# Expert weights laid out by the host, one solid piece of 8 KB per partition and load

## The chip, the cores and the metric

The kernel runs on one core of a Trainium2 chip. The metric is the device time of the whole program in microseconds, the median of three runs. The engines are TensorE (PE, with its weight loads as PEld), VectorE (DVE), ScalarE (ACT), GpSimd (POOL) and SyncE (SP). SP issues every DMA of this kernel; 16 DMA engines carry them.

## The reference

256 tokens of 1024 numbers, all float32, pass through two blocks. The first has a conditioned norm, a mixer (convolution and mLSTM) and a mixture of 32 experts; the second has two layers of attention and a SwiGLU network. The experts are the part that matters here:

```python
def expert_rows(args):
    xb, e = args
    return (jax.nn.silu(xb @ w_e_gate[e]) * (xb @ w_e_up[e])) @ w_e_down[e]
```

`w_e_gate` and `w_e_up` have 1024 x 512 numbers per expert, `w_e_down` 512 x 1024: 6 MB per expert, 192 MB in all, and every expert's weights are read once. Each token goes to two experts; which ones, a router computes on the chip.

## The kernel before

The program is one function, `tile_two_blocks_kernel`. All large weights come in loads of 1 MB into tiles called `raw` of 128 partitions x 2048 numbers. `load` (line 64) takes a buffer and issues the DMA from SP (line 69); `load_k` (line 72) cuts rows `k0*128` to `(k0+k)*128` and `n` columns out of a matrix, with the rows `k*128+p` on partition p.

For the experts, `part` (line 703) calls `load_k`. A gate or up load takes half an expert's matrix, 4 x 128 rows of 512 numbers; each partition gets four pieces of 2 KB that stand 256 KB apart in memory. A down load takes 2 x 128 rows of 1024 numbers: two pieces of 4 KB per partition. That is six loads of 1 MB for each expert, 192 in all. In the stage of the experts there are 16 `raw` buffers, in three pools that take turns (line 691).

Experts are worked in units (`UNITS`, line 36): four units of two experts, then six of four. The first four experts are fixed, the later ones are taken in the order `order`, which is computed on the chip, so from then on SP reads the expert's number into a register (line 700) and the DMA's address comes from it. `load_to` (line 721) issues loads up to 16 ahead of the unit that is worked. For each unit TensorE does `gather` (line 891, every second unit), `gate_up` (line 913, tiles pg and pu), a transpose, `down` (line 954, tile pd), and then `combine` into acc. A group of loads is free when its matmuls are done, and SP waits for that buffer by buffer.

Ahead of the third unit stands `fallback()` (line 850): a branch (line 853) that all engines take, over a loop for the case that an expert got more tokens than its unit has room for. The loop reads the same weights in pieces of its own (lines 871 and 878).

Tiles and tensors in the rows: `raw<-in_w_e_gate_dram` is such a load; xg, pg, pu, hT, pd, acc are the unit's tiles; `in_ada_w_dram` and `in_a_w_qkv_dram` are weights of the second block, loaded by the same `load`.

Of the kernel before, what the change touches and what calls it, by code (L numbers as in the profile page):

```python
# [7 lines left out]
F32 = mybir.dt.float32  # L8
# [12 lines left out]
NE = 32  # L21
# [21 lines left out]
def kernel(ctx: ExitStack, tc: tile.TileContext, I, cst, out):  # L43
    nc = tc.nc
    PE, ACT, DVE, POOL, SP = nc.tensor, nc.scalar, nc.vector, nc.gpsimd, nc.sync
# [10 lines left out]
    def pb(name):  # L56
        return psum.tile([128, 512], F32, name=name, tag="pb", bufs=3)
# [6 lines left out]
    def load(src, k, n):  # L64
        pick = pools["raw"][pools["n"] % len(pools["raw"])]
        pools["n"] += 1
        t = pick.tile([128, 2048], F32, name="raw", tag="raw")
        v = t[:, :k * n].rearrange("p (k n) -> p k n", n=n)
        pools.get("dma", SP).dma_start(out=v, in_=src)  # L69
        return v  # L70

    def load_k(w, k0, k, n0, n):
        return load(w[k0 * 128:(k0 + k) * 128, n0:n0 + n].rearrange("(k p) n -> p k n", p=128), k, n)
# [49 lines left out]
    def mm(o, a, b, first=True, last=True):  # L123
        return PE.matmul(o, a, b, start=first, stop=last, skip_group_check=True)  # L124
# [473 lines left out]
    for i in range(2):  # L598
        ps = pa("hmT")
        for j in range(2):  # L600
            h = 2 * i + j
            for t in range(2):
                PE.transpose(ps[:, j * 256 + t * 128:j * 256 + (t + 1) * 128], hm[:, t, h, :], ident)
            src = ps[:, j * 256:(j + 1) * 256]
# [84 lines left out]
    with tc.tile_pool(name="moe", bufs=1) as pp, \  # L689
# [5 lines left out]
        def expert_loads():  # L695
            for ne, r0 in UNITS:
                w = ewt[r0] = [{}, {}, {}]
                for r in range(r0, r0 + ne):
                    if r not in at:
                        at[r] = nc.values_load(order[0:1, r:r + 1], engines=[mybir.EngineType.SP], min_val=0, max_val=NE - 1,  # L700
                                               skip_runtime_bounds_check_because="a permutation of the experts")

                def part(i, nm, k0, k, n, j):
                    e = at[r0 + j]
                    src = I[nm][0][e] if isinstance(e, int) else I[nm][0][bass.ds(e, 1)].rearrange("e k n -> (e k) n")
                    w[i][k0 // k, j] = load_k(src, k0, k, 0, n)

                for h in range(2):
                    for i, nm in enumerate(("w_e_gate", "w_e_up")):
                        for j in range(ne):  # L710
                            part(i, nm, 4 * h, 4, 512, j)
                            yield
                for h in range(2):
                    for j in range(ne):
                        part(2, "w_e_down", 2 * h, 2, 1024, j)
                        yield

        loads = expert_loads()
        loaded = [0]

# [129 lines left out]
        def fallback():  # L850
            over = nc.values_load(ovi, min_val=0, max_val=1,
                                  skip_runtime_bounds_check_because="a comparison gives zero or one")
            with tc.If(over > 0, preferred_fallthrough_block=False):
                wide = pp.tile([64, 33], F32, name="wide")
                DVE.tensor_scalar(wide[:, 32:33], place, WIDE - 0.5, float(CAP4), op0=ALU.is_lt, op1=ALU.mult)
                DVE.tensor_scalar(wide[0:32, 0:32], ident[0:32, 0:32], wide[0:32, 32:33], None, op0=ALU.mult)
                pw = pb("ovw")[:, 0:32]
                mm(pw, ones[0:32, :], wide[0:32, 0:32])
                wov = pp.tile([128, 2, 32], F32, name="wov")
                for t in range(2):  # L860
                    DVE.tensor_tensor(wov[:, t, :], sl[:, t, :], pw, ALU.subtract)
                    DVE.scalar_tensor_tensor(wov[:, t, :], wov[:, t, :], CAP4 + 0.5, wE[:, t, :], op0=ALU.is_gt, op1=ALU.mult)
                ov = pp.tile([128, 2048], F32, name="ov", tag="xg", bufs=2)
                hid = ov[:, 0:1024].rearrange("p (f t) -> p f t", f=4)
                wg = ov[:, 1024:2048].rearrange("p (k n) -> p k n", n=128)
                wd = ov[:, 1024:1536].rearrange("p (k n) -> p k n", n=128)
                with tc.For_i(0, NE, 1) as e:
                    for f in range(4):
                        ps = pb("ovgu")
                        for j, nm in enumerate(("w_e_gate", "w_e_up")):  # L870
                            SP.dma_start(out=wg, in_=I[nm][0][bass.ds(e, 1), :, f * 128:(f + 1) * 128]
                                         .rearrange("e (k p) n -> p (e k) n", p=128))
                            for k in range(KT):
                                mm(ps[:, j * 256:(j + 1) * 256], wg[:, k, :], h32[:, k, :], k == 0, k == KT - 1)
                        ACT.activation(hid[:, f, :], ps[:, 0:256], AF.Silu)
                        DVE.tensor_tensor(hid[:, f, :], hid[:, f, :], ps[:, 256:512], ALU.mult)
                    for n in range(8):
                        SP.dma_start(out=wd, in_=I["w_e_down"][0][bass.ds(e, 1), :, n * 128:(n + 1) * 128]
                                     .rearrange("e (k p) n -> p (e k) n", p=128))
                        for t in range(2):  # L880
                            ps = pb("ovd")
                            for k in range(4):
                                mm(ps[:, 0:128], hid[:, k, t * 128:(t + 1) * 128], wd[:, k, :], k == 0, k == 3)
                            tmp = pp.tile([128, 512], F32, name="ovt", tag="yl", bufs=2)[:, 0:128]
                            DVE.tensor_tensor(tmp, ps[:, 0:128], gate2[:, n * 128:(n + 1) * 128], ALU.mult)
                            xs = x[:, t, n * 128:(n + 1) * 128]
                            DVE.scalar_tensor_tensor(xs, tmp, wov[:, t, bass.ds(e, 1)], xs, op0=ALU.mult, op1=ALU.add)
# [94 lines left out]
        for u, (ne, r0) in enumerate(UNITS):  # L982
            if u == 2:
                fallback()
                gf = act.tile([128, D], F32, name="gf", tag="gate1")
                SP.dma_start(out=gf, in_=I["g_final"].unsqueeze(0).to_broadcast([128, D]))
            done += 6 * ne
            load_to(done + RAW_BUFS + RAW2_BUFS)
            if u % 2 == 0:
                gr, xg = gather(u)  # L990
            g = slice(128 * (u % 2), 128 * (u % 2) + 128)
            hid = gate_up(ne, ewt[r0], xg[:, :, g])
            if prev:
                prev()
            gT, ws = scatter_of(ne, r0, gr[:, :, g])
            prev = down(ne, ewt[r0], transposed(hid), gT, ws, u == 0, u == len(UNITS) - 1)
            ewt.pop(r0)
# [364 lines left out]
def _constants():  # L1362
# [27 lines left out]
    def ang(pos, half, theta):  # L1390
# [10 lines left out]
    return c  # L1401


_INS = ["x", "c", "w_ada", "b_ada", "g_norm1", "w_in", "b_if", "conv_dw_w", "conv_dw_b", "conv_ln_g", "conv_ln_b",
        "w_conv_out", "qk_conv_w", "qk_conv_b", "m_norm_g", "w_m_out", "w_out", "g_norm2", "w_rg", "b_rg", "w_re",
        "b_re", "w_e_gate", "w_e_up", "w_e_down", "g_final", "c_2", "ada_w_2", "ada_b_2", "norm1_g_2", "norm2_g_2",
        "a_w_qkv_2", "a_w_o_2", "a_lam_q1_2", "a_lam_k1_2", "a_lam_q2_2", "a_lam_k2_2", "a_subln_g_2", "b_w_qkv_2",
        "b_w_o_2", "b_qnorm_g_2", "b_knorm_g_2", "f_w_in_2", "f_w_out_2", "final_g_2"]

# [20 lines left out]
```

## Time and profile before

| | us |
|---|---|
| median of 3 runs | 1456.59 (1455.54 to 1457.0) |
| the profiled execution | 1455.63 |
| its span, first to last instruction | 1453.9 |

The mean granted clock of TensorE in the profiled execution is 0.956 of full speed. The profile comes from one execution; spans and sums are made against 1455.63. Times in the rows below are microseconds from the start of the span. The share of the DMA engines is the time that packets took, over 16 engines; overlapping packets can bring it above 1.

### The profile page before, as it was taken

To read this page: it belongs to the slowest core of one execution; us is meant where nothing else is said; L and a number is where in the kernel's file an instruction comes from. 1 tells how busy PE (TensorE), PEld (TensorE's weight loads), DVE (VectorE), ACT (ScalarE), POOL (GpSimd) and SP (SyncE) were. 2 spreads that over 40 slices of the span, in tenths; PEclk is the share of its full clock that TensorE was granted. 3 is DMA by queue.
4 is the path that set the end of the run, shared out by engine and by line. 5 is a ranking of instruction groups with operands and counts; after the bars stand their busy time and mean duration, and the time that the engine had idled before them with its cause. 6 is when DMAs were issued, how large, how long until landed. Compare 5 with 4: busy or idle time off the path is not lost.

```text
span 1453.9 us, 20075 instructions
## 1 busy us (share of the span) xinstructions
PE 1303.4 (90%) x8125; PEld 888.7 (61%) x8125; DVE 620.3 (43%) x1074; ACT 490.9 (34%) x840; POOL 57.9 (4%) x99
## 2 busy tenths in 40 slices
PE   5799999897997787777778999999999999999997
PEld 1686797634342222121125877698999777799997
DVE  0798856511111011010016545754544765744454
ACT  1465354311010000010006555543443554643442
POOL 0000000000000000000002211000000120000000
PEclk9899999798999899898999999999999999999999
DMA  8987557899999999999999766658555566755500
GB/s 303 401 290 260 197 185 257 310 409 360 392 409 410 414 406 414 410 411 414 408 390 337 257 229 207 244 187 290 174 175 173 203 216 212 285 188 184 174 30 30
DMA packets 200002, 408.83 MB, mean 281 GB/s; under 512 B 10057, under 2 KB 90430, under 8 KB 193762
## 3 DMA queue, kind: packets, MB, share of 16 engines
q1 hardware_dynamic: 199906, 407.51, 76.1%
q8 instruction: 65, 1.06, 0.3%
q14 instruction: 31, 0.25, 0.0%
HBM read 406.43 MB, written 1.05 MB: 280 GB/s over the span
## 4 chain that ended last, share of the span: by engine, by line
PE 74%; DMA 15%; DVE 4%; SPq 3%; issue 2%; ACT 2%; POOL 1%; POOLq 0%; DVEq 0%; ACTq 0%
PE ada L124 5%; DMA raw<-in_w_e_up_dram 5%; PE pu L124 5%; PE pd L124 4%; DMA raw<-in_w_e_down_dram 4%; PE pg L124 4%; PE fu L119 3%; PE fg L120 3%; PE fg L119 3%; PE fg L121 3%; PE fu L120 3%; PE fu L121 3%; PE facc L119 3%; DMA raw<-in_w_e_gate_dram 3%; SPq L69 3%; PE facc L120 3%
## 5 line engine op out<-in xcount | busy, mean ns | idle before, releaser
L92 DVE TENSOR_TENSOR lo<-raw,hi 128x1024 fp32r<-128x1024 f32 x120 | 145.2, 1230 | 126.3 <-ACT hi L90 124.6
L110 DVE TENSOR_TENSOR lo<-raw,hi 128x1024 fp32r<-128x1024 f32 x120 | 146.1, 1224 | 97.0 <-ACT hi L108 96.8
L90 ACT ACTIVATE hi<-raw 128x1024 fp32r<-128x1024 f32 x120 | 125.0, 1061 | 143.9 <-PE facc L121 79.2
L108 ACT ACTIVATE hi<-raw 128x1024 fp32r<-128x1024 f32 x120 | 125.8, 1057 | 123.6 <-issue 55.8
L124 PE MATMUL pu<-raw,xg 128*32 128x512 f32 (+1 forms) x512 | 130.2, 744 | 31.3 <-DMA raw<-in_w_e_up_dram 31.3
L124 PE MATMUL pd<-raw,hT 128*32 128x512 f32 (+1 forms) x512 | 111.1, 597 | 16.7 <-DMA raw<-in_w_e_down_dram 8.8
L124 PE MATMUL pg<-raw,xg 128*32 128x512 f32 (+1 forms) x512 | 109.6, 622 | 17.4 <-DMA raw<-in_w_e_gate_dram 17.4
L926 DVE TENSOR_TENSOR hid<-hid,pu 128x256 f32<-128x256 f32 x20 | 7.5, 418 | 241.9 <-PE pu L124 241.9
L119 PE MATMUL fg<-Hh,lo 128*128 128x256 f32 x352 | 100.7, 286 | 4.3 <-DVE Hh L351 4.3
L124 PE MATMUL ada<-raw,cc 128*32 128x512 f32 x576 | 98.0, 635 | 6.5 <-DMA raw<-in_w_ada_dram 6.5
L124 PEld LDWEIGHTS pu<-raw,xg 128*32 128x32 f32 (+1 forms) x512 | 30.3, 138 | 117.4 <-DMA raw<-in_w_e_up_dram 63.2
L120 PE MATMUL fg<-Hl,hi 128*128 128x256 f32 x352 | 100.4, 285 | 0.9 <-DVE Hl L115 0.9
L119 PE MATMUL fu<-Hh,lo 128*128 128x256 f32 x352 | 100.8, 286 | 0.0
L121 PE MATMUL fg<-Hh,hi 128*128 128x256 f32 x352 | 100.3, 285 | 0.0
L120 PE MATMUL fu<-Hl,hi 128*128 128x256 f32 x352 | 100.3, 285 | 0.0
L121 PE MATMUL fu<-Hh,hi 128*128 128x256 f32 x352 | 100.2, 285 | 0.0
L119 PE MATMUL dense<-hi,Hl 128*128 128x256 f32 x288 | 82.9, 288 | 0.1
L124 PEld LDWEIGHTS pd<-raw,hT 128*32 128x32 f32 (+1 forms) x512 | 30.3, 116 | 84.5 <-issue 58.0
L120 PE MATMUL dense<-lo,Hh 128*128 128x256 f32 x288 | 81.5, 283 | 0.0
L121 PE MATMUL dense<-hi,Hh 128*128 128x256 f32 x288 | 81.4, 284 | 0.0
L124 PEld LDWEIGHTS pg<-raw,xg 128*32 128x32 f32 (+1 forms) x512 | 26.6, 120 | 77.6 <-issue 41.4
L119 PEld LDWEIGHTS fg<-Hh,lo 128*128 128x128 f32 x352 | 68.2, 194 | 6.5 <-issue 4.7
(413 smaller groups left out, 2608.6 us busy)
## 6 DMA issues: line engine op xcount, KB each, us to landing
raw<-in_w_e_gate_dram SPq DMA_DIRECT2D x64, 1024.0 KB
raw<-in_w_e_up_dram SPq DMA_DIRECT2D x64, 1024.0 KB
raw<-in_w_e_down_dram SPq DMA_DIRECT2D x64, 1024.0 KB
raw<-in_ada_w_dram SPq DMA_DIRECT2D x48, 1024.0 KB
raw<-in_f_w_in_dram SPq DMA_DIRECT2D x44, 1024.0 KB
raw<-in_w_ada_dram SPq DMA_DIRECT2D x24, 1024.0 KB
raw<-in_f_w_out_dram SPq DMA_DIRECT2D x22, 1024.0 KB
raw<-in_w_in_dram SPq DMA_DIRECT2D x20, 1024.0 KB
```

Of the source, the lines that this page charges most:

```text
L69: pools.get("dma", SP).dma_start(out=v, in_=src)
L90: ACT.activation(hv, src, AF.Copy)
L92: DVE.tensor_tensor(lv, src, hv.bitcast(F32), ALU.subtract)
L108: ACT.activation(hv, src, AF.Copy)
L110: DVE.tensor_tensor(lv, src, hv.bitcast(F32), ALU.subtract)
L119: PE.matmul(o, al, bh, start=first, stop=False, skip_group_check=True)
L120: PE.matmul(o, ah, bl, start=False, stop=False, skip_group_check=True)
L121: PE.matmul(o, ah, bh, start=False, stop=last, skip_group_check=True)
L124: return PE.matmul(o, a, b, start=first, stop=last, skip_group_check=True)
L926: DVE.tensor_tensor(hid[:, c], hid[:, c], pgu[1][:, c], ALU.mult)
```

## The change

The host builds one array `experts` of (32, 6, 128, 2048) numbers instead of passing the three weight arrays: for each expert the two halves of gate, of up and of down, each already in the form of the tile, so that partition p's 2048 numbers stand in one piece of 8 KB, and a load's 1 MB in one piece too. `part` then loads one such block, into the same tile with the same meaning of its columns. The fallback loop reads its smaller pieces out of the same array, in two halves.

```diff
-                def part(i, nm, k0, k, n, j):
+                def part(i, h, j):
                     e = at[r0 + j]
-                    src = I[nm][0][e] if isinstance(e, int) else I[nm][0][bass.ds(e, 1)].rearrange("e k n -> (e k) n")
-                    w[i][k0 // k, j] = load_k(src, k0, k, 0, n)
+                    src = I["experts"][bass.ds(e, 1), 2 * i + h].rearrange("e p (k n) -> (e p) k n", k=2 if i == 2 else 4)
+                    w[i][h, j] = load(src, src.shape[1], src.shape[2])
...
-                            SP.dma_start(out=wg, in_=I[nm][0][bass.ds(e, 1), :, f * 128:(f + 1) * 128]
-                                         .rearrange("e (k p) n -> p (e k) n", p=128))
+                            for h in range(2):
+                                SP.dma_start(out=wg[:, 4 * h:4 * h + 4, :], in_=I["experts"][bass.ds(e, 1), 2 * j + h]
+                                             .rearrange("e p (k n) -> (e p) k n", k=4)[:, :, f * 128:(f + 1) * 128])
...
+def _experts(inputs):
...
+    parts = []
+    for name, k in (("w_e_gate", 4), ("w_e_up", 4), ("w_e_down", 2)):
+        w = np.asarray(inputs[name])[0]
+        parts.append(w.reshape(NE, 2, k, 128, -1).transpose(0, 1, 3, 2, 4).reshape(NE, 2, 128, 2048))
+    return np.ascontiguousarray(np.concatenate(parts, axis=1))
```

On TensorE, VectorE, ScalarE and GpSimd the order of instructions is the same before and after, row for row. On SP the loads keep their places and waits. The first place is SP at the branch of the fallback, with the waits of each row (DMAHW are the landings of SP's own loads, PE is TensorE). Before:

```order
L69 DMA raw<-in_w_e_gate_dram 128x4x512 [waits DMAHW0_49,PE_49]
L69 ISA
L69 DMA raw<-in_w_e_up_dram 128x4x512 [waits DMAHW1_49,PE_49]
L69 ISA
L69 DMA raw<-in_w_e_up_dram 128x4x512 [waits DMAHW2_49,PE_49]
L851 TENSOR_LOAD ovi [waits DVE_49]
L853 COMPARE_AND_BRANCH
L853 UNCONDITIONAL_BRANCH [waits DMAHW0_49,DMAHW1_49,DMAHW2_49,DMAHW3_49,DMAHW4_49,DMAHW5_49,DMAHW6_49,DMAHW7_49]
```

And now:

```order
L69 DMA raw<-experts_dram 128x2048 [waits DMAHW0_49,PE_49]
L69 ISA
L69 DMA raw<-experts_dram 128x2048 [waits DMAHW1_49,PE_49]
L69 ISA
L69 DMA raw<-experts_dram 128x2048 [waits DMAHW2_49,PE_49]
L851 TENSOR_LOAD ovi [waits DVE_49]
L853 COMPARE_AND_BRANCH
L853 UNCONDITIONAL_BRANCH [waits DMAHW0_49,DMAHW1_49,DMAHW2_49,DMAHW3_49,DMAHW4_49,DMAHW5_49,DMAHW6_49,DMAHW7_49]
```

Nothing moved: each load has the same waits, and its destination has become one piece of 2048 numbers per partition. In both, SP leaves the branch only when all its eight landing counters stand where they should.

The second place is SP inside the fallback loop (tile ov), which a run enters only when an expert overflows. Before:

```order
L871 DMA ov<-in_w_e_gate_dram 128x8x128 [waits DMAHW3_49,DVE_49,Activation_49]
L871 ISA
L871 DMA ov<-in_w_e_up_dram 128x8x128 [waits DMAHW4_49,DMAHW3_49,PE_49]
L871 ISA
L871 DMA ov<-in_w_e_gate_dram 128x8x128 [waits DMAHW5_49,DMAHW4_49,PE_49]
```

And now:

```order
L872 DMA ov<-experts_dram 128x4x128 [waits DMAHW3_49,DVE_49,Activation_49]
L872 ISA
L872 DMA ov<-experts_dram 128x4x128 [waits DMAHW4_49]
L872 ISA
L872 DMA ov<-experts_dram 128x4x128 [waits DMAHW5_49,DMAHW3_49,PE_49]
```

Each load of the loop has become two of half the size.

## Rows read from the trace of the kernel before

**Rows 1.** The page: busy tenths, DMA and GB/s in 40 slices of the span.

```profile
PE   5799999897997787777778999999999999999997
DMA  8987557899999999999999766658555566755500
GB/s 303 401 290 260 197 185 257 310 409 360 392 409 410 414 406 414 410 411 414 408 390 337 257 229 207 244 187 290 174 175 173 203 216 212 285 188 184 174 30 30
```

**Rows 2.** The chain that ended last, expert stage: start us, us, what.

```profile
336.91 14.24 DMA raw<-in_w_e_gate_dram
...
362.74 0.42 PE pg L124
...
375.65 7.09 PE pd L124 x32
...
400.03 7.09 PE pd L124 x32
...
428.15 3.01 PE pu L124 x21
431.16 17.76 DMA raw<-in_w_e_down_dram
...
722.66 13.26 DMA raw<-in_w_e_up_dram
```

**Rows 3.** Windows of the expert stage; the last columns are granted clock, DMA share, GB/s.

```profile
356.00:358.00 2.00, 2.00 (x12) 1.87 (x13) 0.00 (x0) 0.89 (x3) 0.00 (x0) 0.61 1.02 396
358.00:360.00 2.00, 2.00 (x8) 0.61 (x7) 0.00 (x0) 0.86 (x2) 0.00 (x0) 1.00 0.47 180
360.00:362.00 2.00, 2.00 (x12) 0.87 (x13) 0.76 (x2) 0.56 (x1) 0.00 (x0) 1.00 0.11 41
362.00:364.00 2.00, 2.00 (x12) 0.71 (x10) 0.00 (x0) 0.00 (x0) 0.00 (x0) 1.00 0.11 15
364.00:368.00 4.00, 4.00 (x22) 1.30 (x20) 0.00 (x0) 0.00 (x0) 0.00 (x0) 1.00 0.87 306
...
460.00:478.00 18.00, 12.83 (x60) 2.52 (x52) 0.00 (x0) 0.00 (x0) 0.00 (x0) 0.81 1.05 407
740.00:752.00 12.00, 9.72 (x53) 2.68 (x46) 1.44 (x3) 0.00 (x0) 0.00 (x0) 1.00 1.02 418
```

**Rows 4.** Timeline of SP, its load issues: start us, us with waits, what, count.

```profile
362.75 1.03 SPq L69 DMA_DIRECT2D raw<-in_w_e_gate_dram  x2
...
397.48 8.61 SPq L69 DMA_DIRECT2D raw<-in_w_e_gate_dram  x4
```

**Rows 5.** DMA issues between 230 and 362 us.

```profile
raw<-in_w_e_gate_dram SPq DMA_DIRECT2D x14, 1024.0 KB
raw<-in_w_e_up_dram SPq DMA_DIRECT2D x14, 1024.0 KB
raw<-in_w_e_down_dram SPq DMA_DIRECT2D x12, 1024.0 KB
```

**Rows 6.** DMA queue (packets, MB, share of 16 engines) and issues between 362.5 and 740 us.

```profile
q1 hardware_dynamic: 65483, 153.79, 103.5%
...
raw<-in_w_e_down_dram SPq DMA_DIRECT2D x52, 1024.0 KB
raw<-in_w_e_gate_dram SPq DMA_DIRECT2D x50, 1024.0 KB
raw<-in_w_e_up_dram SPq DMA_DIRECT2D x50, 1024.0 KB
```

**Rows 7.** DMA packets in 460 to 478 us, 430 to 446 us, 44 to 60 us.

```profile
DMA packets 3687, 7.32 MB, mean 407 GB/s; under 512 B 112, under 2 KB 112, under 8 KB 3687
...
DMA packets 1742, 6.73 MB, mean 421 GB/s; under 512 B 98, under 2 KB 98, under 8 KB 1742
...
DMA packets 3599, 6.52 MB, mean 408 GB/s; under 512 B 98, under 2 KB 3189, under 8 KB 3189
```

**Rows 8.** One window with few loads in flight, those of ada weights in 8 KB pieces.

```profile
227.00:231.00 4.00, 4.00 (x37) 4.00 (x36) 1.57 (x3) 0.86 (x2) 0.00 (x0) 1.00 0.99 371
```

More of the change, by code (lines that the diff above doesn't have):

```diff
@@ L701, in expert_loads @@
                                                skip_runtime_bounds_check_because="a permutation of the experts")
-                def part(i, nm, k0, k, n, j):
+                def part(i, h, j):
                     e = at[r0 + j]
-                    src = I[nm][0][e] if isinstance(e, int) else I[nm][0][bass.ds(e, 1)].rearrange("e k n -> (e k) n")
-                    w[i][k0 // k, j] = load_k(src, k0, k, 0, n)
+                    src = I["experts"][bass.ds(e, 1), 2 * i + h].rearrange("e p (k n) -> (e p) k n", k=2 if i == 2 else 4)
+                    w[i][h, j] = load(src, src.shape[1], src.shape[2])
                 for h in range(2):
-                    for i, nm in enumerate(("w_e_gate", "w_e_up")):
+                    for i in range(2):
                         for j in range(ne):
-                            part(i, nm, 4 * h, 4, 512, j)
+                            part(i, h, j)
                             yield
@@ L714, in expert_loads @@
                     for j in range(ne):
-                        part(2, "w_e_down", 2 * h, 2, 1024, j)
+                        part(2, h, j)
                         yield
@@ L869, in fallback @@
                         ps = pb("ovgu")
-                        for j, nm in enumerate(("w_e_gate", "w_e_up")):
-                            SP.dma_start(out=wg, in_=I[nm][0][bass.ds(e, 1), :, f * 128:(f + 1) * 128]
-                                         .rearrange("e (k p) n -> p (e k) n", p=128))
+                        for j in range(2):
+                            for h in range(2):
+                                SP.dma_start(out=wg[:, 4 * h:4 * h + 4, :], in_=I["experts"][bass.ds(e, 1), 2 * j + h]
+                                             .rearrange("e p (k n) -> (e p) k n", k=4)[:, :, f * 128:(f + 1) * 128])
                             for k in range(KT):
@@ L877, in fallback @@
                     for n in range(8):
-                        SP.dma_start(out=wd, in_=I["w_e_down"][0][bass.ds(e, 1), :, n * 128:(n + 1) * 128]
-                                     .rearrange("e (k p) n -> p (e k) n", p=128))
+                        for h in range(2):
+                            SP.dma_start(out=wd[:, 2 * h:2 * h + 2, :], in_=I["experts"][bass.ds(e, 1), 4 + h]
+                                         .rearrange("e p (k n) -> (e p) k n", k=2)[:, :, n * 128:(n + 1) * 128])
                         for t in range(2):
@@ L1401, in _constants @@
     return c
+def _experts(inputs):
+    import numpy as np
+    parts = []
[3 more added lines that the diff above has]
+    return np.ascontiguousarray(np.concatenate(parts, axis=1))
 _INS = ["x", "c", "w_ada", "b_ada", "g_norm1", "w_in", "b_if", "conv_dw_w", "conv_dw_b", "conv_ln_g", "conv_ln_b",
         "w_conv_out", "qk_conv_w", "qk_conv_b", "m_norm_g", "w_m_out", "w_out", "g_norm2", "w_rg", "b_rg", "w_re",
-        "b_re", "w_e_gate", "w_e_up", "w_e_down", "g_final", "c_2", "ada_w_2", "ada_b_2", "norm1_g_2", "norm2_g_2",
+        "b_re", "g_final", "c_2", "ada_w_2", "ada_b_2", "norm1_g_2", "norm2_g_2",
         "a_w_qkv_2", "a_w_o_2", "a_lam_q1_2", "a_lam_k1_2", "a_lam_q2_2", "a_lam_k2_2", "a_subln_g_2", "b_w_qkv_2",
@@ L1422 @@
         aps[name] = nc.dram_tensor(f"in_{name}_dram", a.shape, mybir.dt.from_np(a.dtype), kind="ExternalInput").ap()
+    arrays["experts_dram"] = _experts(inputs)
+    aps["experts"] = nc.dram_tensor("experts_dram", (NE, 6, 128, 2048), F32, kind="ExternalInput").ap()
     arrays["constants_dram"] = _constants()
```

## Prediction

> **What bounds the kernel now.** I read the page first, then the stages by window, then the chain of waits, and last the DMA queue in the few stretches where one size of piece moves alone. [rows 1] shows two kinds of stage. In slices 9 to 21 of 40 (36.3 us each, the experts) the DMA engines show 9 and move 390 to 414 GB/s, but for slice 10 with 360, while PE shows mostly 7; from slice 23 on PE shows 9 and DMA drops to 5 to 8. So a cheaper load can pay in the expert stage alone. TensorE over the whole span (90%) tells nothing about that stage.
>
> The expert stage is itself three stretches.
>
> - *283 to 345 us.* The chain is TensorE with almost no break; the first 16 loads were fetched ahead. A faster load is not waited for here. The step "DMA raw<-in_w_e_gate" at 336.91, 14.24 us long, ends at 351.15, where PE goes on with the next gather [rows 2]; a gather reads no weights, and before it PE stands in the branch of line 853. I count that step as the branch, not as a load.
> - *345 to 364 us.* SP also meets that branch, and there it waits for every load that it has issued (first order piece above). DMA runs dry: 396, 180, 41 and 15 GB/s in four steps of 2 us [rows 3]. SP's next load goes out at 362.75 [rows 4], and the chain has TensorE's matmuls pg ending at 362.74 [rows 2]: it is a buffer freed by TensorE that it waited for. After this TensorE is the chain without a break until 431 [rows 2].
> - *364 to some 752 us.* DMA is never idle: its queue's share is 103.5% of 16 engines from 362.5 to 740 us [rows 6], 1.05 and 1.02 in two windows of it [rows 3] (packets overlap a little, so a full engine reads over 1). From 431 the chain hangs on loads that take 13 to 18 us from issue to landing, because they stand behind others [rows 2]. Here the time is the number of loads times the time of one. [rows 6] counts them: 52 down, 50 gate and 50 up; with the 40 before [rows 5] that is all 192.
>
> After the last down load there are PE's last matmuls, the norms and the second block; the order of instructions on all engines is the same there, so this tail simply follows.
>
> **What one piece costs.** Between 460 and 478 us only gate and up loads move: 3687 packets, 112 of them small, so 3575 pieces of 2 KB in 18 us. 16 engines x 18,000 ns / 3575 = 80.6 ns for a piece. Between 430 and 446 only down loads: 1742 - 98 = 1644 pieces of 4 KB in 16 us, 155.7 ns each [rows 7]. The second 2 KB cost 75.1 ns, the first 80.6: a piece costs about 5.5 ns and then 75.1 ns for 2 KB. Drawn on to 8 KB: 155.7 + 2 x 75.1 = 305.9 ns. A load of 1 MB in 128 pieces gives every engine 8, so 2.447 us, against 32 x 80.6 = 2.579 us for gate and up and 16 x 155.7 = 2.491 us for down.
>
> The trace holds 8 KB pieces too (the ada weights), never alone in a full queue. Between 44 and 60 us they mix with 1 KB pieces: 3599 packets, 3189 under 2 KB, of which 98 are small, so 3091 of 1 KB and 410 of 8 KB [rows 7]. With 43.0 ns for 1 KB (the same line drawn back), 256 us of engine time less 132.9 leaves 300 ns for a piece of 8 KB. I take the cheap bound from it: 300 ns, a load of 2.40 us. The dear bound is that nothing is gained past 4 KB: 2 x 155.7 = 311.4 ns, 2.491 us. I take 305.9, which lies between.
>
> The Trainium skill, page "DMA: Bandwidth & Descriptors", section "Specifications", gives 512 B as the smallest transfer for line rate. By that rule 2 KB pieces lose nothing and the change brings 0 us. [rows 7] does not agree: 407 GB/s with 2 KB and 421 with 4 KB in full queues.
>
> **The change part by part.**
>
> - *Gate and up loads, 100 of them in the full stretch:* 2.579 - 2.447 = 0.132 us each, 13.2 us.
> - *Down loads, 52:* 2.491 - 2.447 = 0.044 us each, 2.3 us.
> - *The 40 loads before 362 us* (28 gate and up, 12 down [rows 5]): they get cheaper by at most 28 x 0.132 + 12 x 0.044 = 4.2 us, and I count none of it. The cover is TensorE's chain, unbroken by loads up to 431 [rows 2]; the queue only runs dry some 4 us sooner, at about 356, and then waits for the same buffer at 362.75. Without that cover the whole 4.2 us would be gained.
> - *SP's own time.* Four issues take SP 8.61 us in the full stretch, 2.2 us each, and two take 1.03 us where the queue is empty [rows 4]. Fewer pieces may let SP run further ahead, up to its 16 buffers. That moves no byte sooner while the engines are full: 0 us. Its waits and its order are the same (first order piece).
> - *The fallback loop* gets 32 loads per expert where 16 were (second order piece). It is skipped in this run: the 192 loads of [rows 5, 6] are all there are. 0 us.
> - *TensorE's side:* the same matmuls on the same numbers. Its own pace is shown where it did not wait: from 375.65 to 400.03, one unit of 12 loads in 24.4 us [rows 2], 2.03 us a load. That unit has two experts; it stays under 2.447. So loads stay what is waited for.
>
> Sum: 13.2 + 2.3 = 15.5 us. The profiled execution took 1455.63 us (span 1453.9 and 1.7 around it), 0.96 under the median of the three runs. 1455.63 - 15.5 = 1440.1; set against the median, 1441.1 us.
>
> A measurement of this kernel tells about 0.2% (2.9 us) from no change.
>
> **The rivals.** Their times are set against the median.
>
> - *No gain past 4 KB.* A piece of 8 KB would cost as two of 4 KB. Then gate and up gain 100 x (2.579 - 2.491) = 8.8 us, down nothing: 1447.8 us. For it speaks that no stretch has 8 KB pieces alone at the full rate; against it the mixed stretch of [rows 7], which left no more than 300 ns. The Trainium skill, same page, section "Why small descriptors are slow (HBM only)", names a fixed cost of about 3 cycles for each packet beside one for each 32 B. By it (an estimate: 67, 131 and 259 cycles for 2, 4 and 8 KB) gate and up would gain 3.4%, down 1.1%, together some 10 us, near this rival; [rows 7] shows a larger fixed cost, 5.5 ns of 80.6.
> - *The early loads pay too, or 8 KB is cheaper still.* If SP at 362.75 waited for its own loads (it does wait for them in the branch) and TensorE's end at 362.74 only fell together with it, the 4.2 us come on top: 1436.9. With 300 ns a piece instead of 305.9 (2.400 us a load) the sum is 100 x 0.179 + 52 x 0.091 = 22.6 us: 1434.0. Against the first: TensorE's chain runs on past 362 with no wait for a load.
> - *Slower: long pieces that start 8 KB apart read worse.* Every load becomes one solid MB, and the 16 engines walk it side by side. No load of before has that shape. The slowest rows with 8 KB pieces are 227 to 231 us, 371 GB/s at a share of 0.99 [rows 8]: 1.0486 MB / 371 GB/s = 2.826 us a load, and 152 x 2.826 - (100 x 2.579 + 52 x 2.491) = +42 us, so 1498.6. The point where it decides: a mean load of 387.4 / 152 = 2.549 us, 411 GB/s. Against it: at 227 us there were few loads in the queue, 2 KB pieces go at 306 in such a place too (364 to 368 [rows 3]), and down loads read a solid stretch already, at 421.
> - *No change:* 1456.6. It needs something other than the loads to set the stretch from 431 on; the DMA share of 103.5% [rows 6] speaks against it. The first rule cited above would give this time.
>
> **How the numbers follow.** The forecast (1438.5 to 1444.5) has 0.62; the early loads or a cheaper piece 0.13; no gain past 4 KB 0.12; no change 0.05; slower 0.08. Faster is 0.62 + 0.13 + 0.12 = 0.87, same 0.05, slower 0.08. For the range I leave out the slow case, no change, and the far end of the cheap one: 1436 to 1448.5 holds the forecast, most of the next and the 4 KB case. The prediction is that of the likeliest case, 1441.1.
>
> **What the next profile would show.** Right: DMA at 425 to 430 GB/s with a share near 1.02 in the stretch from some 364 us to the end of the expert loads; that end near 737 instead of 752; 128 packets of 8 KB per load; the dry spot at 356 to 364 a few us longer, and SP's next load again at about 362.7; TensorE's waits for loads 2.45 us apart; the time from the last down load to the end unchanged. The first step is wrong if the full stretch stays at 421 or falls under 411; the step on the early loads is wrong if SP's load after the branch goes out at 359 or before. The prediction as a whole fails if DMA shows gaps in the full stretch, which would mean that buffers, not bytes, set the pace.

## The result, and the profile after

The changed kernel took 1440.8 us (median of 4 runs, 1440.68 to 1442.87) against 1456.07 for the kernel before (4 runs, 1455.43 to 1457.0): a ratio of 0.9889, 95% interval 0.9876 to 0.9903. Forecast were 1441.1 us and 1436 to 1448.5. The changed kernel was profiled again later beside other runs of before: 1444.55 against 1455.91, ratio 0.9918 (0.9906 to 0.9931). So the gain is 15.3 us by the first pair of medians and 11.4 by the second; what lies between is taken up below.

The slices of the page after (TensorE, DMA, GB/s, then the packets of the whole execution) answer to [rows 1]. In slices 12 to 20, counted from 1 as in the prediction, DMA now moves 425 or 426 GB/s, where it moved 406 to 414; the packets are 142,658.

```profile
PE   5799999897997777677769999999999999999997
...
DMA  8987557798899999999989666757554665855500
GB/s 303 403 287 258 196 193 264 305 415 374 375 426 425 426 425 426 426 426 425 426 347 366 225 216 224 261 185 273 172 194 144 223 226 195 297 185 176 175 30 30
DMA packets 142658, 408.83 MB, mean 284 GB/s; under 512 B 10057, under 2 KB 90430, under 8 KB 111842
```

Windows of the expert stage after (the last three columns are granted clock, DMA share and GB/s) answer to [rows 3]:

```profile
354.00:356.00 2.00, 2.00 (x10) 2.00 (x11) 0.00 (x0) 0.86 (x2) 0.00 (x0) 0.50 0.82 340
356.00:358.00 2.00, 2.00 (x11) 2.00 (x11) 0.00 (x0) 1.03 (x3) 0.00 (x0) 0.50 0.19 74
358.00:360.00 2.00, 2.00 (x10) 0.74 (x9) 0.00 (x0) 1.29 (x3) 0.00 (x0) 0.99 0.00 0
360.00:362.00 2.00, 2.00 (x11) 1.02 (x12) 0.76 (x2) 0.57 (x1) 0.00 (x0) 1.00 0.01 4
362.00:364.00 2.00, 2.00 (x14) 0.58 (x10) 0.00 (x0) 0.00 (x0) 0.00 (x0) 1.00 0.10 16
364.00:368.00 4.00, 4.00 (x22) 1.43 (x20) 0.00 (x0) 0.00 (x0) 0.00 (x0) 1.00 0.89 358
...
460.00:478.00 18.00, 10.78 (x52) 2.35 (x56) 0.00 (x0) 0.00 (x0) 0.00 (x0) 0.89 1.01 425
500.00:600.00 100.00, 76.16 (x388) 21.48 (x388) 8.94 (x21) 5.93 (x12) 0.00 (x0) 0.93 1.01 425
```

The dry spot is longer and starts sooner: counted against this kernel's full rate of 426 GB/s it loses some 8.6 us of DMA time; the one in [rows 3], counted against the 407 there, loses 5.9. It still ends at the same moment. SP's next load, on its timeline (start, us with waits, what, count), goes out 0.16 us later than in [rows 4]:

```profile
362.91 1.18 SPq L69 DMA_DIRECT2D raw<-experts_dram  x2
```

The DMA queue from 362.5 to 740 us answers to [rows 6], a third of the packets for the same loads (two loads of a_w_qkv and one of ada_w come with them):

```profile
q1 hardware_dynamic: 22135, 159.49, 100.4%
...
raw<-experts_dram SPq DMA_DIRECT2D x152, 1024.0 KB
```

The chain of waits after, beside [rows 2]:

```profile
336.29 15.06 DMA raw<-experts_dram
...
352.03 1.83 PE gath L124 x7
...
407.67 0.57 PE gath L124 x4
408.24 17.59 DMA raw<-experts_dram
...
702.95 19.55 DMA raw<-experts_dram
...
722.62 19.57 DMA raw<-experts_dram
...
742.23 3.64 PE pd L124 x20
```

TensorE is the chain up to 408 us; from there it is loads, but for one stretch of 20 us from 485 on, a unit's down and the next gather. Two steps on loads start 19.67 us apart, and SP has 8 loads under way by then: 2.459 us a load, where 2.447 was forecast.

**Three marks.** To tell where a difference lies I read three moments in every trace: the first matmul on expert weights (tile pg, 64 columns), the first one of the fifth unit (pg, 32 columns), and the start of the last one on expert weights (pd). Up to the fifth unit a unit has two experts, from there four. The lines give min/median/max ns and the first and last start. Before:

```profile
L124 PE MATMUL pg<-raw,xg x16: 592/592/643, 289.3 to 294.5; 128*64 128x512 f32 x16
...
L124 PE MATMUL pg<-raw,xg x34: 592/592/617, 412.1 to 420.3; 128*32 128x512 f32 x34
...
L124 PE MATMUL pd<-raw,hT x64: 589/592/617, 743.7 to 758.9; 128*32 128x512 f32 x64
```

After:

```profile
L124 PE MATMUL pg<-raw,xg x16: 592/592/706, 289.6 to 294.9; 128*64 128x512 f32 x16
...
L124 PE MATMUL pg<-raw,xg x34: 592/592/617, 412.7 to 420.8; 128*32 128x512 f32 x34
...
L124 PE MATMUL pd<-raw,hT x35: 592/592/617, 734.6 to 745.3; 128*32 128x512 f32 x35
```

The table has the same for all kernels of this study, from one profile each; A is the first mark, A to B and B to C the stretches between marks, and the rest is the span behind C.

| kernel | A | A to B | B to C | A to C | rest |
|---|---|---|---|---|---|
| before | 289.3 | 122.8 | 346.8 | 469.6 | 695.0 |
| changed | 289.6 | 123.1 | 332.6 | 455.7 | 695.8 |
| after_again (changed, second profile) | 290.2 | 122.8 | 332.9 | 455.7 | 694.8 |
| gate_up_only | 287.6 | 123.4 | 334.6 | 458.0 | 696.7 |
| down_only | 288.4 | 123.0 | 344.4 | 467.4 | 695.4 |
| pieces_2k | 289.5 | 122.4 | 354.6 | 477.0 | 696.7 |
| pieces_4k | 287.7 | 123.0 | 338.1 | 461.1 | 696.7 |
| far_pitch | 292.2 | 122.9 | 332.6 | 455.5 | 695.0 |
| early_old | 291.4 | 122.3 | 334.8 | 457.1 | 696.4 |
| early_new | 289.7 | 123.0 | 346.5 | 469.5 | 695.3 |
| before_no_fallback | 287.7 | 119.9 | 343.4 | 463.3 | 698.5 |
| after_no_fallback | 290.8 | 120.1 | 330.8 | 450.9 | 696.8 |
| fallback_pool | 289.6 | 123.0 | 332.6 | 455.6 | 696.8 |
| fallback_u6 | 293.8 | 123.7 | 338.9 | 462.6 | 695.4 |

From A to C the change gains 13.9 us, in both profiles of the changed kernel, and all of it behind B.

### The profile page after: what moved, and what is told of

Same layout as the page of the kernel before. It is cut to its first block, busy times and chain, and to the rows that moved or that the text cites. A ratio compares the mean times of both kernels' runs of the same rounds, so it can differ in the third digit from the quotient of the medians.

```text
span 1441.1 us, 20075 instructions
## 1 busy us (share of the span) xinstructions
PE 1292.9 (90%) x8125; PEld 889.5 (62%) x8125; DVE 620.7 (43%) x1074; ACT 491.0 (34%) x840; POOL 58.0 (4%) x99
## 4 chain that ended last, share of the span: by engine, by line
PE 67%; DMA 25%; DVE 3%; issue 2%; ACT 1%; POOL 1%; SPq 0%; POOLq 0%; DVEq 0%; ACTq 0%
DMA raw<-experts_dram 23%; PE ada L124 6%; PE fg L120 3%; PE fu L119 3%; PE fg L119 3%; PE fg L121 3%; PE fu L120 3%; PE fu L121 3%; PE facc L119 3%; PE facc L120 3%; PE facc L121 3%; PE pd L124 2%; PE dense L119 2%; PE dense L120 2%; PE dense L121 2%; PE pu L124 2%
## 5 line engine op out<-in xcount | busy, mean ns | idle before, releaser
L108 ACT ACTIVATE hi<-raw 128x1024 fp32r<-128x1024 f32 x120 | 125.9, 1057 | 122.3 <-issue 55.8
L124 PE MATMUL pu<-raw,xg 128*32 128x512 f32 (+1 forms) x512 | 108.7, 638 | 29.8 <-DMA raw<-experts_dram 29.8
L124 PE MATMUL pg<-raw,xg 128*32 128x512 f32 (+1 forms) x512 | 117.5, 690 | 17.5 <-DMA raw<-experts_dram 17.5
L966 DVE SCALAR_TENSOR_TENSOR pd<-pd,ws,gate 128x512 f32<-128x512 f32 x20 | 15.2, 759 | 133.1 <-PE pd L124 132.1
```

Of the source, the lines that this page charges most:

```text
L108: ACT.activation(hv, src, AF.Copy)
L966: DVE.scalar_tensor_tensor(pd, pd, ws, gate2[:, n * 512:(n + 1) * 512], op0=ALU.mult, op1=ALU.mult)
```

## The experiments

The theory at the start: the time of the full stretch is the number of pieces times the cost of a piece, and a piece costs a few ns whatever its length. The first rivals: it is not the length but the order in memory; or the single array; or that SP can run further ahead.

**gate_up_only and down_only: one part of the change each.** Gate and up alone from the new array:

```diff
-                    src = I["experts"][bass.ds(e, 1), 2 * i + h].rearrange("e p (k n) -> (e p) k n", k=2 if i == 2 else 4)
-                    w[i][h, j] = load(src, src.shape[1], src.shape[2])
+                    if i < 2:
+                        src = I["experts"][bass.ds(e, 1), 2 * i + h].rearrange("e p (k n) -> (e p) k n", k=2 if i == 2 else 4)
+                        w[i][h, j] = load(src, src.shape[1], src.shape[2])
+                    else:
+                        src = I["w_e_down"][0][bass.ds(e, 1)].rearrange("e k n -> (e k) n")
+                        w[i][h, j] = load_k(src, 2 * h, 2, 0, 1024)
```

> Gate and up from the new array in 8 KB pieces, down from its own array in 4 KB pieces as before. Theory (the time of the full stretch is the number of pieces times the cost of a piece): 100 x 0.132 = 13.2 us of the gain stay, so 1442.9 us; worked from the changed kernel's 1440.8 and its measured 2.4715 us a load, 52 x (2.491 - 2.4715) = 1.0 us is lost, 1441.8. Rival (what helps is that one array with one pitch holds all loads, or that SP can run ahead all the time): with every third load of the old kind a good part of the 15 us is lost, 1446 or more.

Measured: 1443.47 us, ratio to before 0.9913 (0.9895 to 0.9932), before 1456.4 in this set. A to C is 11.6 us shorter than before. down_only is the same edit the other way round:

> Down from the new array in 8 KB pieces, gate and up from their own arrays in 2 KB pieces as before. Theory: 52 x 0.044 = 2.3 us gained, 1453.8 us (by the measured 2.4715 us a load only 1.0 us, 1455.1). Rival (SP's running ahead or the single array is what helps): 1450 or less.

Measured: 1456.01 us, ratio 0.9988 (0.9976 to 1.0); A to C 2.2 us shorter. The two parts add up, 11.6 + 2.2 = 13.8 to the whole 13.9, and each stands near its term (13.2 and 2.3). The rival that a mixture loses the gain falls. In the medians down_only shows hardly anything: 2 us is less than runs of one kernel differ.

**pieces_2k and pieces_4k: the length of a piece alone.** In pieces_2k the host leaves 512 B free after every 2 KB of a row, so that no two blocks are neighbours; in pieces_4k it stores a tile as two halves. The load's destination is written in as many pieces (not shown).

In pieces_2k:

```diff
-                    src = I["experts"][bass.ds(e, 1), 2 * i + h].rearrange("e p (k n) -> (e p) k n", k=2 if i == 2 else 4)
+                    src = I["experts"][bass.ds(e, 1), 2 * i + h].rearrange("e p b n -> (e p) b n")[:, :, 0:512]
...
-    return np.ascontiguousarray(np.concatenate(parts, axis=1))
+    w = np.concatenate(parts, axis=1).reshape(NE, 6, 128, 4, 512)
+    return np.concatenate([w, np.zeros((NE, 6, 128, 4, 128), w.dtype)], axis=4)
```

In pieces_4k:

```diff
-                    src = I["experts"][bass.ds(e, 1), 2 * i + h].rearrange("e p (k n) -> (e p) k n", k=2 if i == 2 else 4)
+                    src = I["experts"][bass.ds(e, 1), 2 * i + h].rearrange("e b p n -> (e p) b n")
...
-        parts.append(w.reshape(NE, 2, k, 128, -1).transpose(0, 1, 3, 2, 4).reshape(NE, 2, 128, 2048))
+        parts.append(w.reshape(NE, 2, k, 128, -1).transpose(0, 1, 3, 2, 4).reshape(NE, 2, 128, 2, 1024).transpose(0, 1, 3, 2, 4))
```

> The changed kernel's order in memory, but each row of 8 KB is cut in four by gaps of 512 B, so that all 152 loads of the full stretch, down too, move in pieces of 2 KB. Theory: 152 x 2.579 us instead of 152 x 2.4715, 16.3 us more than the changed kernel, 1457; counted from the kernel before, 52 x (2.579 - 2.491) = 4.6 us more, 1460.7. Full stretch near 407 GB/s, 80 to 81 ns a piece. Rival (the order in memory, all of a partition's numbers side by side, is what helps, not the length of a piece): 1441 to 1444.

> Each load is two solid halves of 512 KB, 4 KB per partition in each, so that all 152 loads of the full stretch move in pieces of 4 KB. Theory with the predicted line (305.9 ns for 8 KB, 155.7 for 4): 152 x 0.044 = 6.7 us more than the changed kernel, 1447.5. Theory with the measured 2.4715 us a load: 152 x (2.491 - 2.4715) = 3.0 us more, 1443.8. Rival (no gain past 4 KB): 1441, as the changed kernel.

Measured: pieces_2k 1464.33 us, ratio to before 1.0044 (1.0028 to 1.0061), slower than before; pieces_4k 1449.08, ratio 0.9945 (0.993 to 0.996). From A to C pieces_4k takes 5.4 us more than the changed kernel, between its two theories (6.7 and 3.0). pieces_2k misses its expectation (1457, or 1460.7 counted from before): from A to C it takes 21.3 us more than the changed kernel and 7.4 more than before. Some 3.4 us of both lie at the branch, where SP's next load goes out 76.8 us behind A, in the kernel before 73.5 and in the changed one 73.3:

```profile
366.37 0.58 SPq L70 DMA_DIRECT2D raw<-experts_dram  x1
```

SP leaves the branch there at 363.4; for the 3 us up to this issue the profile shows no wait, and what fills them stays open. The other 4 us against before are about what the down loads now cost more, 52 x (2.576 - 2.491) = 4.4 (2.576 us is 1.0486 MB at the 407 GB/s below). Packets between 460 and 478 us in pieces_2k:

```profile
DMA packets 3673, 7.31 MB, mean 406 GB/s; under 512 B 111, under 2 KB 111, under 8 KB 3672
```

in pieces_4k:

```profile
DMA packets 1971, 7.57 MB, mean 421 GB/s; under 512 B 122, under 2 KB 122, under 8 KB 1971
```

and in the changed kernel:

```profile
DMA packets 1056, 7.65 MB, mean 425 GB/s; under 512 B 122, under 2 KB 122, under 8 KB 122
```

Small ones taken off and worked out as in the prediction, a piece costs 80.9, 155.8 and 308.4 ns for 2, 4 and 8 KB. From 500 to 600 us, where 1 MB after another moves without a break, the rows are, for pieces_2k:

```profile
500.00:600.00 100.00, 75.49 (x370) 23.03 (x374) 8.94 (x21) 7.56 (x14) 0.00 (x0) 0.94 1.05 407
```

and for pieces_4k:

```profile
500.00:600.00 100.00, 75.36 (x395) 22.20 (x395) 8.94 (x21) 5.86 (x11) 0.00 (x0) 0.95 1.03 420
```

407, 420 and (above) 425 GB/s. B to C is 354.6, 338.1 and 332.6 us: halving the number of pieces gains 16.5, of which 3.4 are the late restart above, halving it again 5.5. So there is a gain past 4 KB, and the rival "no gain past 4 KB" falls. But the second step is under half of the first, and a fixed cost from such pairs is not one number: 2 x 80.9 - 155.8 = 6.0 ns, then 2 x 155.8 - 308.4 = 3.2. "A constant for each piece" is good to some 3 ns in 300.

**far_pitch: the order in memory alone.**

```diff
-                    src = I["experts"][bass.ds(e, 1), 2 * i + h].rearrange("e p (k n) -> (e p) k n", k=2 if i == 2 else 4)
+                    src = I["experts"][bass.ds(e, 1), :, 2 * i + h].rearrange("e p (k n) -> (e p) k n", k=2 if i == 2 else 4)
...
-    return np.ascontiguousarray(np.concatenate(parts, axis=1))
+    return np.ascontiguousarray(np.concatenate(parts, axis=1).transpose(0, 2, 1, 3))
```

> The same 8 KB pieces, but the six tiles of an expert lie side by side in a partition's row, so a load's 128 pieces start 48 KB apart and its MB is no longer solid. Theory (only the length of a piece counts): 1441 us, 425 GB/s in the full stretch, as in the changed kernel. Rival (the solid MB is part of the gain): 1446 or more, under 420 GB/s.

Measured: 1444.5 us, ratio 0.9914 (0.9898 to 0.993). The whole time lies between the two expectations and would have left it open. The window does not:

```profile
500.00:600.00 100.00, 75.33 (x391) 22.09 (x392) 8.93 (x21) 5.87 (x11) 0.00 (x0) 0.95 1.01 426
```

426 GB/s, and A to C is 455.5 against 455.7. What this profile has more lies ahead of the experts (A at 292.2). Whether a load's MB is solid plays no part here.

**before_no_fallback and after_no_fallback: both kernels without the branch.** These would not cover an input that needs the fallback.

```diff
             if u == 2:
-                fallback()
                 gf = act.tile([128, D], F32, name="gf", tag="gate1")
```

> The kernel before without the call of the fallback, so neither TensorE nor SP meets its branch (the loop that it guards does not run in this case; an input that needs it would not be covered). The queue lost some 6 us in the dry spot (356 to 368 us: full time less what moved). Theory (DMA sets the time from 407 us on, and idle DMA time before that is lost): 1456.4 - 6 = 1450. Rival (TensorE's chain up to 407 sets the start of the full stretch): TensorE saves its 6 us in the branch too, but less than 3 us come through, 1453 to 1456.

> The changed kernel without the call of the fallback. Here the dry spot is longer, some 9.5 us of DMA time between 354.5 and 366. Theory: 1441 - 9.5 = 1431.5, so that the change would be worth 18.5 to 19.5 us without the branch, the early loads' 4 us with it. Rival (the early loads are covered by TensorE's chain with or without the branch): the two kernels without the fallback differ by 15 to 16 us, as those with it do.

Measured: before_no_fallback 1450.31 us, ratio to before 0.9963 (0.9946 to 0.9979); after_no_fallback 1440.35, ratio 0.9889 (0.9875 to 0.9904). For before_no_fallback the theory held (1450 forecast): its dry spot of 5.9 us is gone, A to C is 6.3 us shorter, and the rival's 1453 to 1456 falls. For after_no_fallback it failed: the two kernels differ by 10 us, not 19, and from A to C by 12.4. The rival's 15 to 16 is missed too. The windows of after_no_fallback show why:

```profile
412.00:416.00 4.00, 3.89 (x19) 2.40 (x19) 1.71 (x7) 0.56 (x1) 0.00 (x0) 1.00 1.01 422
416.00:418.00 2.00, 2.00 (x21) 0.68 (x25) 0.00 (x0) 0.00 (x0) 0.00 (x0) 1.00 0.54 225
418.00:420.00 2.00, 2.00 (x24) 0.61 (x20) 0.00 (x0) 0.00 (x0) 0.00 (x0) 1.00 0.26 53
420.00:422.00 2.00, 2.00 (x24) 0.56 (x20) 0.00 (x0) 0.00 (x0) 0.00 (x0) 1.00 0.76 287
422.00:424.00 2.00, 2.00 (x24) 0.65 (x20) 0.00 (x0) 0.00 (x0) 0.00 (x0) 1.00 1.00 422
```

Without the branch the queue of 8 KB pieces runs dry all the same, later: DMA is faster than TensorE in the units of two experts, all 16 buffers are full, and the next load waits until TensorE gives one back (3.4 us lost). So of the changed kernel's 8.6 us only 5.2 go, and A to C is 4.8 us shorter. In before_no_fallback DMA never stops there, and A to B is the same 119.9 and 120.1 us. So I formed another theory: *up to the fifth unit TensorE sets the time, and DMA can be ahead by no more than 16 buffers; only behind it do loads count.*

**early_old and early_new: the two halves of the loads.** The first 40 loads from one layout, the 152 behind them from the other; early_old is shown, early_new has `== False` and with it the two branches exchanged, and after_again is the changed kernel as it is.

```diff
+                    if (count[0] < 40) == True:
+                        src = I[("w_e_gate", "w_e_up", "w_e_down")[i]][0][bass.ds(e, 1)].rearrange("e k n -> (e k) n")
+                        w[i][h, j] = load_k(src, 2 * h, 2, 0, 1024) if i == 2 else load_k(src, 4 * h, 4, 0, 512)
+                    else:
+                        src = I["experts"][bass.ds(e, 1), 2 * i + h].rearrange("e p (k n) -> (e p) k n", k=2 if i == 2 else 4)
+                        w[i][h, j] = load(src, src.shape[1], src.shape[2])
+                    count[0] += 1
```

> The first 40 loads (28 gate and up, 12 down, up to the dry spot at the branch) come from the old arrays in pieces of 2 and 4 KB, the 152 behind them from the new one in 8 KB. Theory (up to the fifth unit TensorE sets the time, so what the first 40 loads cost does not show): the changed kernel's time to within 1 us, 1441, and SP's first load behind the branch at the same distance from the first expert matmul, 73.3 us. Rival (the early loads carry their share of the gain): 4 us more, 1445.

> The other half: the first 40 loads in 8 KB pieces, the 152 behind them old. Theory: nothing gained, 1455.5 to 1457. Rival: 4 us gained, 1452.

> The changed kernel itself on the same chip as the two halves, as what they are set against: 1440 to 1443. The first matmul on expert weights began anywhere between 287 and 294 us in the profiles so far, in kernels that do the same up to there, so a part of the spread between runs should lie ahead of the experts: from that matmul to the end this run should take 1151 to 1152 us, whatever its whole time.

Measured: early_old 1442.91 us (ratio 0.9906, 0.9892 to 0.992), early_new 1455.77 (0.9996, 0.9986 to 1.0007), after_again 1444.55 (0.9918, 0.9906 to 0.9931). The first 40 loads in the new layout alone bring nothing, in A to C either (469.5 against 469.6); without them 12.5 of 13.9 us stay. early_old misses its expectation a little: 1.4 us of the early loads' 4.2 do show, 2.2 more behind B less 0.8 ahead of it. SP's next load went out 74.3 us behind A there, where 73.3 was expected. The trace tells why: SP stands in the branch until its last load has landed, at 365.0 (its eight waits there, ns min/median/max, first and last start),

```profile
L860 SPq EVENT_SEMAPHORE  x8: 17/17/17, 359.6 to 365.0; - x8
```

and sends the next one at 365.77 without a wait for a buffer. The dearer early loads hold it 1.0 us past the moment at which the buffer lets it go in the changed kernel. after_again took 1150.5 us from A to the end (expected 1151 to 1152, 1151.5 in the first profile).

**fallback_u6: the branch where loads are waited for.**

```diff
-            tc.tile_pool(name="raw2", bufs=3) as raw2, tc.tile_pool(name="raw3", bufs=5) as raw3:
+            tc.tile_pool(name="raw2", bufs=3) as raw2, tc.tile_pool(name="raw3", bufs=4) as raw3:
...
-        h32 = pp.tile([128, KT, T], F32, name="h32", tag="xg", bufs=2)
+        h32 = pp.tile([128, KT, T], F32, name="h32")
...
+            if u == 6:
+                fallback()
             if u == 2:
-                fallback()
```

> The changed kernel with the fallback met ahead of the seventh unit of experts instead of the third, some 520 us, where loads are waited for; its input then has a buffer of its own, and one of the 16 landing buffers goes for it. Theory: SP again waits for all that it has issued, but buffers stand free when it leaves, so the dry spot is some 3 us instead of 9.5, and TensorE's 6 us in the branch lie in its waits for loads: 1434 to 1436. Rival (15 buffers instead of 16, or a queue that has to fill up from nothing, cost as much): 1440 or more.

Measured: 1451.79 us, ratio to before 0.9958 (0.9944 to 0.9972); A to C is 6.9 us longer than in the changed kernel. The theory failed, and the rival's 1440 or more came. Its windows at the branch:

```profile
544.00:546.00 2.00, 2.00 (x14) 0.29 (x6) 0.00 (x0) 0.66 (x2) 0.00 (x0) 1.00 0.77 324
546.00:548.00 2.00, 0.64 (x3) 0.14 (x2) 0.00 (x0) 0.00 (x0) 0.00 (x0) 1.00 0.11 45
548.00:550.00 2.00, 0.42 (x1) 0.00 (x0) 0.00 (x0) 0.00 (x0) 0.00 (x0) 0.94 0.01 4
550.00:552.00 2.00, 0.00 (x0) 0.00 (x0) 0.00 (x0) 0.00 (x0) 0.00 (x0) 0.50 0.37 66
552.00:554.00 2.00, 0.00 (x0) 0.00 (x0) 0.00 (x0) 0.00 (x0) 0.00 (x0) 0.50 0.86 340
```

(324 + 45 + 4 + 66 + 340) / 426 x 2 = 3.7 us of transfer in 10: 6.3 us lost, twice the 3 that I expected, and B to C is 6.3 us longer than in the changed kernel. By the bytes landed the two kernels are level ahead of it (70.1 and 70.3 loads at 150 us behind A) and 2.7 loads apart behind it (148.6 and 151.3 at 350 us). What the missing branch gained up to the fifth unit was lost ahead of that, in a second dry spot at B, 7.1 us of DMA time between 416 and 430, most of it here:

```profile
420.00:424.00 4.00, 3.89 (x28) 1.67 (x30) 0.98 (x6) 0.00 (x0) 0.00 (x0) 1.00 0.08 35
424.00:430.00 6.00, 6.00 (x64) 1.81 (x60) 0.00 (x0) 0.00 (x0) 0.00 (x0) 1.00 0.58 199
```

It is the one of after_no_fallback, twice as long; how much of it the missing buffer makes was not separated. So a dry spot costs about its length at either place: 6.3 us cost 6.3 here, and 5.9 cost 6.3 at the old place in the kernel before. I had expected the new place to be the cheaper one. (A to B is 123.7 here without the branch in it, where the kernels without a branch have 120. TensorE waits for no load between A and B in any of them; its instructions stand in another order here, with products into acc between those into pu.)

**fallback_pool: SP kept out of the branch.** The loads inside the fallback's loop are issued by GpSimd, and SP's branch then carries no wait for its loads.

```diff
-                                SP.dma_start(out=wg[:, 4 * h:4 * h + 4, :], in_=I["experts"][bass.ds(e, 1), 2 * j + h]
+                                nc.gpsimd.dma_start(out=wg[:, 4 * h:4 * h + 4, :], in_=I["experts"][bass.ds(e, 1), 2 * j + h]
...
-                            SP.dma_start(out=wd[:, 2 * h:2 * h + 2, :], in_=I["experts"][bass.ds(e, 1), 4 + h]
+                            nc.gpsimd.dma_start(out=wd[:, 2 * h:2 * h + 2, :], in_=I["experts"][bass.ds(e, 1), 4 + h]
```

> The changed kernel with the loads inside the fallback's loop issued by GpSimd instead of SP, so that SP no longer waits at the branch for all that it has issued; TensorE still meets the branch and its 6 us. Theory (TensorE sets the time up to the fifth unit, and a dry spot there costs only what the queue then lacks at 412 us): the dry spot at 355 to 364 us goes, but the first expert matmul to that of the fifth unit stays at 122 to 124 us, and of the 332.6 us behind it at most 2 go: 1439 to 1441 in all. Rival (the dry spot is idle DMA time that the end feels): 6 to 9 us less, 1432 to 1435.

Measured: 1443.95 us, ratio 0.9911 (0.9892 to 0.9929), A to C 455.6: the changed kernel's. But the dry spot did not go, as theory and rival both had it, so this run does not decide between them:

```profile
356.00:358.00 2.00, 2.00 (x13) 2.00 (x12) 0.00 (x0) 1.03 (x3) 0.00 (x0) 0.60 0.24 94
358.00:360.00 2.00, 1.98 (x9) 0.50 (x7) 0.00 (x0) 1.19 (x3) 0.00 (x0) 1.00 0.00 0
360.00:362.00 2.00, 2.00 (x11) 1.02 (x12) 0.76 (x2) 0.56 (x1) 0.00 (x0) 1.00 0.00 0
362.00:364.00 2.00, 2.00 (x12) 0.72 (x10) 0.00 (x0) 0.00 (x0) 0.00 (x0) 1.00 0.25 33
```

and SP's next load stands on its timeline where it stood:

```profile
362.78 1.17 SPq L69 DMA_DIRECT2D raw<-experts_dram  x2
```

SP waits for nothing of its own now and still sends it at 362.78, after 21.4 us of waiting for TensorE's pg. It is the buffer that TensorE frees late, because TensorE itself stood in the branch. For the changed kernel that settles the point that the prediction had only argued; how it was in the kernel before is told below.

No whole kernel of this study beats the changed one; after_no_fallback does from A to C, by 4.8 us, and lacks a part.

## Why the prediction was right

- *What bounds the stages.* Right. A to B, the units of two experts, is 122.3 to 123.4 us in all eleven profiles that have the branch in it, with pieces of 2, 4 or 8 KB: TensorE's time. Behind B the stretch follows the loads. Its ends were read 4 to 5 us early: the last load lands at 755.9 before and 742.2 after, not at 752 and 737.
- *The cost of a piece.* The mechanism is shown (pieces_2k, pieces_4k, far_pitch), the size a little off. Forecast were 425 to 430 GB/s and 2.447 us a load; measured 425 to 426 and 2.459 by the chain. 152 x 0.012 = 1.8 us, and that is about what the sum of 15.5 has too much against the 13.9 from A to C. The step at fault is "Drawn on to 8 KB": the line through 2 and 4 KB flattens, and 8 KB costs 307 to 308 ns instead of 305.9. The cheap bound of 300 ns, taken from a stretch with mixed pieces, lay on the wrong side of the line; of the dear bound, 311.4, something was true.
- *Gate and up 13.2, down 2.3.* Measured one by one from A to C: 11.6 and 2.2.
- *The 40 early loads at nothing.* Right to 1.4 us (early_old), but the reading behind it was half wrong, and that it came out was in part luck. The prediction has SP wait for a buffer at 362.75. In the kernel before, SP's eight waits for its own landings in the branch (first and last start) ended at 362.0, and the load went out 0.7 us later with no wait for a buffer. In the changed kernel they ended at 359.1, and only there SP then waited for the buffer, 3.1 us. Before:

```profile
L853 SPq EVENT_SEMAPHORE  x8: 17/17/17, 356.5 to 362.0; - x8
```

After, with SP's longest wait for pg between 356 and 368 us in the last column:

```profile
L853 SPq EVENT_SEMAPHORE  x8: 17/17/17, 353.8 to 359.1; - x8
...
SPq L69 <- PE pg L124: 3.4, 2, 3.1
```

So SP did wait for its own loads, as the rival on the early loads had it, and TensorE's end at 362.74 only fell together with it. The 4.2 us were not gained because the buffer came free almost at that moment: with cheap early loads before old ones (early_new) SP's load goes out 73.2 us behind A, in the kernel before 73.5. Had TensorE freed it 3 us sooner, the early loads would have paid about that much (an estimate from these rows). What they saved went into the dry spot, 8.6 us instead of 5.9.

- *SP's own time and a deeper queue at nothing.* Loads do stay under way longer (below), and no time came of it: shortly after the dry spot, from 380 to 400 us, DMA already moves 426 GB/s, when by the trace (bytes issued less bytes landed) 3 to 7 MB are under way, 4.7 in the median; the kernel before has 4.1 there and moves 407. It moves the same 426 later with 7.0. That a deep queue is without effect was not tried by itself.
- *The fallback's loads.* Not run, as forecast. The rest behind the experts is unchanged, 695.0 and 695.8 us.
- *The Trainium skill*, page "DMA: Bandwidth & Descriptors", section "Why small descriptors are slow (HBM only)", gives a fixed cost of about 3 cycles a packet; the estimate of some 10 us in the prediction stood on it. The runs show 13.9 us.

The agreement of 1440.8 with 1441.1 is better than the working earned. Two comparisons gave 15.3 and 11.4 us where both profiles show 13.9 from A to C. What differs besides lies mostly ahead of the experts: A falls between 287.6 and 293.8 us, in kernels that do the same work up to there. By the trace SP's 37th issue already varies from 31.0 to 35.1 us; in far_pitch, fallback_u6 and early_new another 1.6 us come in between 128 and 138. Why, is open.

## What to carry to other kernels

Where DMA engines are full, count pieces: two stretches that each hold one length of piece give the cost of the next length to about 1%, but expect a little less than the line promises. Idle DMA time cost about its length wherever it lay, but before pricing its end ask what the queue will wait for next: of 8.6 us, 3.4 came back a little later, as all buffers were full. Loads that get cheaper ahead of a dry spot only make it longer, when something other than these loads sets its end. For effects of a few us compare marks inside the trace, not whole times.

## What the runs showed that I had not expected

Loads are under way for very different times by their pieces. The chain's last long step (start, us) is 13.2 us in pieces_2k:

```profile
729.24 13.21 DMA raw<-experts_dram
```

and 17.75 in pieces_4k:

```profile
728.00 17.75 DMA raw<-experts_dram
```

and 19.57 in the changed kernel (above). Divided by the time of a load (1.0486 MB at 407, 420 and 425 GB/s: 2.576, 2.497 and 2.467 us) that is 5.1, 7.1 and 7.9 loads in the queue. With 8 KB, SP is let go after 0.33 us an issue by the trace, and not after 2.2 us as in [rows 4]. That the number of pieces limits the queue at 2 and 4 KB fits this; it was not tried. What holds it at 8 loads is seen: each load waits for one of SP's eight landing counters (the waits DMAHW0 to DMAHW7 in the order ahead), which is the landing of the load eight places before it. From 420 to 700 us the changed kernel has this wait 112 times (us in total, times, longest):

```profile
SPq L69 <- DMA raw<-experts_dram: 208.0, 112, 2.7
```

In the kernel before, SP's list of waits for the same stretch has none on a load.

The skip of a loop that is not entered stops TensorE for long: its compare and branch (line 853) takes 6.1 us by the trace, up to the gather at 352.03, and in fallback_u6 it does nothing from 550 to 554. After it has stood still so, the granted clock reads 0.50, the lower level (1.2 GHz), and 0.99 from 358 us on. The Trainium skill, page "Runtime: NRT & Kernel Launch", section "Instruction fetch mechanics", says that a taken branch out of the window in hand has to fetch its target first; no run here separates that fetch from the rest of the stop.

The full rate of 426 GB/s with 8 KB pieces is near a ceiling that the Trainium skill names, page "DMA: Bandwidth & Descriptors", section "Where 436 GB/s comes from": 435 GB/s for the ports. No run here tried longer pieces.
